# Eight raw weight buffers instead of six, from mixer tiles that share buffers, and the root of the first norm per token in columns of two

## The chip, the cores and the metric

The kernel runs on one core of a Trainium2 chip. Its time is the device time of one execution in microseconds (us); the time that counts is the median of several executions. A core has five engines with a queue of instructions each, which they run in order: PE (matmuls, with its weight loads shown as PEld), DVE and ACT (elementwise work), POOL and SP. Here SP's queue does nothing but issue DMAs, and POOL has almost no work.

## What is computed

One layer of a decoder trunk on 256 tokens of width 2048, all in f32: a SwiGLU feed-forward network (FFN) of inner width 5632, a mixer with two branches, a second FFN, and a final norm. Every sublayer starts with an RMS norm whose gain and shift come from a vector c.

```python
mods = (c_act @ ada_w[l] + ada_b[l]).reshape(b, N_MOD, d)
h = _modulate(x, ffn1_norm[l], mods[:, 0], mods[:, 1])
x = x + 0.5 * mods[:, 2][:, None, :] * _swiglu(h, ffn1_w_gate[l], ffn1_w_up[l], ffn1_w_down[l])
h = _modulate(x, mix_norm[l], mods[:, 3], mods[:, 4])
y = _hybrid_mixer(h, cos, sin, w_in[l], gdn_conv_w[l], gdn_a_log[l], gdn_dt_bias[l], gdn_norm_w[l],
...
x = x + mods[:, 5][:, None, :] * y
h = _modulate(x, ffn2_norm[l], mods[:, 6], mods[:, 7])
x = x + 0.5 * mods[:, 8][:, None, :] * _swiglu(h, ffn2_w_gate[l], ffn2_w_up[l], ffn2_w_down[l])
return _rms_norm(x, final_norm)
```

where `_hybrid_mixer` is a gated delta rule in 8 heads and a sparse attention in 8 heads, merged by gates and projected by w_out, and `_rms_norm` multiplies by rsqrt(mean(x*x) + 1e-6) over the 2048 channels of a token.

## The kernel before

**Layout.** Activations lie transposed: 16 tiles (KT = 16) of 128 channels by 256 tokens, in `xT`. Weights stream from HBM once, nearly 570 MB in all.

**The weight path.** A load puts 512 KB (128 partitions by 1024 f32) into a buffer with the tag `raw`; there are RB = 6 of them, used in turn. Every f32 product is made of three products at the PE's faster f32r type: ACT copies the load to `whi` (L186, L357), DVE subtracts that from the load to give `wlo` (L187, L358), and PE multiplies `whi` with both halves of the activations and `wlo` with the first half (L196, L198; L363 in the blocked form). `whi` and `wlo` have WB = 3 buffers each. The subtraction is the last reader of a raw buffer, so DVE's progress frees it, and the next load into it, which stands in SP's queue, waits for that. The same six buffers serve the gain and shift matrices `ada_w`: two loads of 512 KB for each tile of 128 of their 18432 columns (L241), each read by one DVE multiply-and-sum (L248) that gives a column of `modc`. These are spread between the weights of the first FFN, the mixer and the start of the second FFN by counters (`pace`, `paces`).

**Order.** The code is written for one stream, and a planner of the framework orders each engine's instructions from its own estimate of when operands and buffers are ready. Pools of tiles with a tag and a count of buffers add waits: a tile takes the place of the one that had its tag `bufs` tiles earlier, once that one has been read for the last time.

**The start** (`start`, L426). ACT squares the 16 tiles of x, PE sums them over the channels by a product with ones, 128x256 wide, so each of the 128 partitions holds all 256 tokens' sums. DVE makes the root by an integer guess and three Newton steps (`rsqrt`, L273) on 128x256, while the first 16 `ada_w` loads go through it. Then each tile is modulated (`modulated`, L318) to an `hpair`, and the gate and up weights run in four passes over 4 of the 16 channel tiles each, 22 of 44 units (NS = 22); partial sums lie in `sums`. The other units and the down projections follow with all 16 channel tiles at a time. Later norms, in `Entry.run` and at the end, do it otherwise: sums per token by a product with a column of ones (`token_sums`, L296), the root on 128x2, and two products that carry it back to all 256 columns (`inv_rms`, L302).

**The mixer** has its own pool `mp`. Four groups of two heads run the delta net (`gdn_group`), while projections (`win`, by `proj`) of the next group, and the compression of keys and values (`compress`, tile `cat`), go on beside them; `gdn_out` gates a group's result by way of `sg` into `oA`. Attention follows in two groups (`attend`): keys `kk`, values `vt`, rotated queries `qr`, probabilities `pr`, transposed `pT`. Then `merge_gates` makes the 16 tiles of merge gates from 32 projections. They are put into the buffers of tiles no longer used, by the list `mtags`; AHEAD = 10 of them are made before the up-projections `wup`, the others between those. The planner also places the four stores of x to HBM (`xd`, L571) in SP's queue.

Of the kernel before, what the change touches and what calls it, by code (L numbers as in the profile page):

```python
# [18 lines left out]
F32 = mybir.dt.float32  # L19
# [3 lines left out]
AF = mybir.ActivationFunctionType  # L23
OP = mybir.AluOpType
# [3 lines left out]
P = 128  # L28
S = 256
D = 2048  # L30
KT = D // P
# [4 lines left out]
AB = 33  # L36
H = 8
WB = 3
RB = 6
TB = 6  # L40
MM = 3
NS = 22
# [10 lines left out]
EPS = 1e-6  # L53
# [51 lines left out]
def trunk(tc, a, out, stage=99, dbg=None):  # L105
    nc = tc.nc
    ctx = ExitStack()
    with ctx:
# [5 lines left out]
        def ptile(shape=(P, 512), dt=F32, tag="c", bufs=7 - MM):  # L114
            return psum.tile(list(shape), dt, tag=tag, name=tag, bufs=bufs)
# [14 lines left out]
        ones = cf[:, C_ONE:C_ONE + P]  # L130
# [11 lines left out]
        for hf in range(2):  # L142
            row = wp.tile([1, HC], F32, tag="raw", name="crow", bufs=RB)
            nc.scalar.dma_start(row, a["c"][:, hf * HC:(hf + 1) * HC])
            for q in range(0, HC, 512):
                pt = ptile()
# [126 lines left out]
        def rsqrt(pool, v, tag):  # L273
            sh = list(v.shape)
            y = pool.tile(sh, F32, tag=tag + "y", name=tag + "y", bufs=2)
            t = pool.tile(sh, F32, tag=tag + "t", name=tag + "t", bufs=2)
            nc.vector.tensor_scalar(y.bitcast(I32), v.bitcast(I32), -0.5, float(0x5F3759DF),
                                    op0=OP.mult, op1=OP.add)
            for it in range(3):
                nc.vector.tensor_mul(t, y, y)  # L280
                nc.vector.scalar_tensor_tensor(t, t, 0.25 ** it, v, op0=OP.mult, op1=OP.mult)
                nc.vector.scalar_tensor_tensor(y, t, -3.0, y, op0=OP.add, op1=OP.mult)
            return y


        nrm = ctx.enter_context(tc.tile_pool(name="nrm", bufs=1))
# [15 lines left out]
        def inv_rms(pt):  # L302

            v = nrm.tile([P, 2], F32, tag="v", name="v", bufs=2)
            nc.vector.tensor_scalar(v, pt[:, 0:2], 1.0 / D, EPS, op0=OP.mult, op1=OP.add)
            r = rsqrt(nrm, v, "nr")
            pb = ptile()
            for j in range(2):
                nc.tensor.matmul(pb[:, j * P:(j + 1) * P], r[:, j:j + 1].to_broadcast([P, P]), ident,
                                 start=True, stop=True)  # L310
            return pb[:, :S]
# [113 lines left out]

        def start(fp, n, sizes, wgu, gain):  # L426
            A = nrm.tile([P, KT], F32, tag="A", name="A", bufs=2)
            pt = ptile((P, S))
            for d in range(KT):
                sq = tmp()  # L430
                nc.scalar.activation(sq, xT[:, d], AF.Square)
                nc.tensor.matmul(pt, ones, sq, start=(d == 0), stop=(d == KT - 1))
            hT = []
            sums = [fp.tile([P, 2, S], F32, tag="a", name="gu", bufs=AB) for _ in range(n - RES)]
            pairs = []
            with tc.tile_pool(name="sp", bufs=1) as sp:
                def mods(k0, kb):
                    for m in (1, 0):
                        for d in range(k0, k0 + kb):
                            for _ in ada_cols(m, d, k0 == 0):  # L440
                                yield
                    yield
                    gains(A, gain, 1, slice(k0, k0 + kb))
                    for d in range(k0, k0 + kb):
                        hT.append(modulated(d, rb, A, 0))
                    yield

                def unit(f, subs):
                    if f in kept:
                        ps = kept[f]  # L450
                    elif f >= n - RES:
                        ps = kept[f] = ptile((P, 2, S))
                    else:
                        ps = ptile((P, 2, S), tag="mm", bufs=MM)
                    here = f in kept
                    last = subs[-1][0] + subs[-1][1] == KT
                    for k0, kb in subs:
                        block_rows(ps, (wgu[f],), hT, k0, kb, k0 == (0 if here else subs[0][0]),
                                   k0 + kb == (KT if here else subs[-1][0] + subs[-1][1]))
                    if not here:  # L460
                        if subs[0][0] == 0:
                            nc.scalar.activation(sums[f], ps, AF.Copy)
                        else:
                            nc.vector.tensor_add(sums[f], sums[f], ps)  # L464
                    if last:
                        gu = ps if here else sums[f]
                        s = tmp()
                        nc.scalar.activation(s, gu[:, 0], AF.Silu)
                        nc.vector.tensor_mul(s, gu[:, 1], s)
                        pair = fp.tile([P, 2, S], F32R, tag="a", name="apair", bufs=AB)  # L470
                        split(pair, s)
                        pairs.append(pair)

                kept = {}
                extra = pace(LT, n - 1)
                offs = [[(sum(sum(z) for z in sizes[:b]) + sum(z[:i]), z[i]) for i in range(len(z))]
                        for b, z in enumerate(sizes)]
                for kt, _ in enumerate(mods(*offs[0][0])):
                    if kt == KT - 5:
                        v = nrm.tile([P, S], F32, tag="ssq", name="vb", bufs=1)  # L480
                        nc.vector.tensor_scalar(v, pt, 1.0 / D, EPS, op0=OP.mult, op1=OP.add)
                        rb = rsqrt(sp, v, "rb")
                for b in range(len(sizes)):
                    todo = offs[b + 1] if b + 1 < len(sizes) else []
                    gen = (None for sub in todo for _ in mods(*sub))
                    step = pace(sum(4 * kb + 2 for _, kb in todo), n - LAG)
                    for f in range(n):
                        unit(f, offs[b])
                        for _ in range(step()):
                            next(gen, None)  # L490
                        if b + 1 == len(sizes):
                            ada(extra())
                            if f == n // 2:
                                late_consts()
            return hT, pairs, ()
# [90 lines left out]
        with ExitStack() as mx:  # L586
            mp = mx.enter_context(tc.tile_pool(name="mp", bufs=1))
# [13 lines left out]
            def one(tag="q", bufs=12):  # L601
                return mp.tile([P, S], F32, tag=tag, name=tag, bufs=bufs)
# [12 lines left out]
            nc.vector.tensor_scalar(gnw, V["gnw"], 0.5, None, op0=OP.mult)  # L615


            sm = mp.tile([P, S], F32, name="sm")
            both(win(0), sm)
            tok = mp.tile([P, 2, P], F32, name="tok")  # L620
            ge = mp.tile([P, 2, 2, 8], F32, name="ge")
# [82 lines left out]
            def gdn_group(h0, q, k, v):  # L704
# [14 lines left out]
                def squares(src, acc):  # L719
                    for j in range(4):  # L720
# [3 lines left out]
                pt = flip(k)  # L724
                squares(pt, ss[:, 0])
                kd = big("kd", 2, (P, 2, P))
                nc.vector.tensor_mul(kd, pt[:, 0:2], per(ekd, 0, h0))
                kE = big("kE", 1, (P, 2, P))
                nc.vector.tensor_mul(kE, pt[:, 2:4], per(egc, 1, h0))
                pt = flip(q)  # L730
# [13 lines left out]
                                 skip_group_check=True)  # L744
# [3 lines left out]
                Dt = bt("Dt")  # L748
# [5 lines left out]
                N = bt("N")  # L754
                for j in range(4):
                    nc.vector.scalar_tensor_tensor(N[:, j], pk[:, j], nC[:, j:j + 1], Dt[:, j],
                                                   op0=OP.mult, op1=OP.mult)
# [20 lines left out]
                for lv in range(1, 6):  # L778
# [26 lines left out]
                    if lv == 1:  # L805
                        pt = flip(v)
# [10 lines left out]
                pt = ptile((64, 4, 64))  # L817
                for j in range(4):
                    nc.tensor.transpose(pt[:, j], z[lo, j, lo], ident[lo, lo])
                zq = mp.tile([P, 4, 64], F32, tag="zq", name="zq", bufs=1)  # L820
                nc.scalar.activation(zq[lo], pt, AF.Copy)
                pp = ptile((P, 4, 64))
                for j in range(4):
# [12 lines left out]
                vn = bt("vn")  # L836
                pv = [ptile((P, 2, P)) for _ in range(2)]
                for p in range(2):
                    for i in range(2):
                        nc.tensor.matmul(pv[p][:, i], z[:, 2 * p + i], Vt[:, 2 * p + i], start=(i == 0),  # L840
                                         stop=(p == 0), skip_group_check=True)
# [44 lines left out]
            def gdn_out(h0, oT):  # L886
                for i in range(2):
                    h = h0 + i
                    zg = both(win(W_GZ + h))
                    th = tmp()  # L890
                    nc.scalar.activation(th, zg, AF.Tanh, scale=0.5)
                    sg = mp.tile([P, S], F32, tag="sg", name="sg", bufs=1)
                    nc.vector.scalar_tensor_tensor(sg, th, 1.0, zg, op0=OP.add, op1=OP.mult)
                    sv = sg.rearrange("p (a b) -> p a b", a=2)
                    nc.vector.tensor_mul(sv, sv, v4(oT)[:, :, i])
                    oA[h] = big("oA", 8, (P, 2, S), F32R)
                    split(oA[h], sg)
# [5 lines left out]

            def compress():
                for b in range(2):
                    cat = mp.tile([P, 2, S], F32, tag="cat", name="cat", bufs=2)
                    for g in range(2):
                        both(win(W_KV + 2 * b + g, False), cat[:, g])
                        yield
# [172 lines left out]

            op_ = oA + oB
            yf = []
            mtags = ["kE", "Dt", "N", "o", "vn", "oT", "kd", "kd", "cat", "cat"] + ["pr", "pr", "kk", "kk", "vt", "vt"]
            sgs = []

            def merge_gates(d):
# [3 lines left out]
                nc.scalar.activation(sg, sg, AF.Tanh, scale=0.5)  # L1092
                sgs.append(sg)

            AHEAD = 10
            for d in range(AHEAD):
                merge_gates(d)
            for d in range(KT):
# [124 lines left out]
```

## Time and profile before

| | |
|---|---|
| median of 3 runs | 2404.76 us (2402.72 to 2405.74) |
| profiled execution | 2399.2 us, of it the span from first to last instruction 2397.4 us |
| PE busy | 2301.0 us, 96% of the span |
| DVE busy | 1781.4 us, 74% |
| ACT busy | 1133.5 us, 47% |
| moved by DMA | 571.00 MB, mean 238 GB/s |

In time the kernel is: the start and the blocked passes of the first FFN to about 300 us, the rest of the first FFN to about 800, the delta net to about 1170, attention to about 1295, merge gates, up-projections and w_out to about 1640, the second FFN, and the final norm from about 2370 us.

How to read the rows below. In a row of instructions stand the start in us, the duration in us, engine, line, operation, out<-in, shape and count, and in brackets how long the engine was idle before it and what ended that. SPq and ACTq are the sequencers of those engines, which issue DMAs. A row of waits reads: who waited, for whom, us in total, times, the longest. A busy PE is no PE at its peak, since matmuls overlap in a pipeline; the count of matmuls in a window tells its pace better.

### The profile page before, as it was taken

How to read it: one execution, taken by the hardware profiler on the slowest of the kernel's cores; microseconds unless marked ns; L12 is line 12 of the kernel's file. 1: busy time of each engine (PE TensorE's matmuls, PEld its weight loads, DVE VectorE, ACT ScalarE, POOL GpSimd, SP SyncE). 2: the span in 40 equal slices, each digit the busy share in tenths (PEclk: the TensorE clock that was granted, in tenths of full speed). 3: DMA queues.
4: the chain of work that ended last, by engine and by line, in shares of the span. 5: the costliest groups of instructions: out<-in, count | busy, mean ns of one | idle time of the engine just before them, and what ended most of it. 6: DMA issues, size and time to landing. Idle time of an engine off the chain costs nothing.

```text
span 2397.4 us, 38975 instructions
## 1 busy us (share of the span) xinstructions
PE 2301.0 (96%) x15094; PEld 2029.9 (85%) x15094; DVE 1781.4 (74%) x2896; ACT 1133.5 (47%) x1787; POOL 1.4 (0%) x8
## 2 busy tenths in 40 slices
PE   6999999999999999999999999999999999999997
PEld 4999987887778888887778888889888888888886
DVE  6888877777777797778887778879666666555555
ACT  3433544433444474554545444556544444344453
POOL 0000000000000000000000000000000000000000
PEclk8999999999999999999999999999999999999999
DMA  9988678888888745547676888666777777665663
GB/s 320 319 299 301 199 260 286 285 289 286 273 291 268 245 158 188 170 151 249 226 252 214 284 290 283 214 218 216 232 242 243 241 243 219 192 195 189 184 191 123
DMA packets 174493, 571.00 MB, mean 238 GB/s; under 512 B 17890, under 2 KB 18146, under 8 KB 174308
## 3 DMA queue, kind: packets, MB, share of 16 engines
q1 hardware_dynamic: 173584, 566.09, 72.0%
q8 instruction: 118, 1.93, 0.3%
q10 hardware_dynamic: 724, 2.43, 0.3%
q14 instruction: 67, 0.55, 0.1%
HBM read 564.25 MB, written 4.19 MB: 237 GB/s over the span
## 4 chain that ended last, share of the span: by engine, by line
PE 62%; DMA 17%; DVE 12%; ACT 5%; issue 4%; ACTq 0%; DVEq 0%; SPq 0%
PE mm L196 34%; PE mm L198 18%; DMA raw<-in_w1gu_dram 9%; PE mm L363 5%; DVE wlo L187 4%; DMA raw<-in_win_dram 4%; ACT whi L186 3%; DMA raw<-in_w1d_dram 2%; DVE adaraw L248 2%; PE c L363 2%; DVE wlo L358 1%; ACT whi L357 1%; DMA raw<-in_wup_dram 0%; DVE gu L464 0%; PE c L799 0%
## 5 line engine op out<-in xcount | busy, mean ns | idle before, releaser
L196 PE MATMUL mm<-hpair,whi 128*128 128x512 f32 x3536 | 1249.9, 394 | 17.2 <-ACT whi L186 8.9
L187 DVE TENSOR_TENSOR wlo<-raw,whi 128x1024 fp32r<-128x1024 f32 (+1 forms) x666 | 796.5, 1197 | 485.1 <-ACT whi L186 477.0
L186 ACT ACTIVATE whi<-raw 128x1024 fp32r<-128x1024 f32 (+1 forms) x666 | 690.6, 1038 | 800.3 <-PE mm L196 268.3
L198 PE MATMUL mm<-hpair,wlo 128*128 128x256 f32 x3536 | 1009.4, 286 | 20.7 <-DVE wlo L187 20.2
L196 PEld LDWEIGHTS mm<-hpair,whi 128*128 128x128 f32 x3536 | 667.5, 189 | 161.3 <-ACT whi L186 13.3
L198 PEld LDWEIGHTS mm<-hpair,wlo 128*128 128x128 f32 x3536 | 671.7, 190 | 37.4 <-DVE wlo L187 34.8
L196 PE MATMUL mm<-apair,whi 128*128 128x512 f32 x1408 | 490.2, 391 | 0.8 <-ACT whi L186 0.8
L198 PE MATMUL mm<-apair,wlo 128*128 128x256 f32 x1408 | 398.3, 283 | 2.0 <-DVE wlo L187 1.9
L196 PEld LDWEIGHTS mm<-apair,whi 128*128 128x128 f32 x1408 | 265.1, 188 | 56.5 <-ACT whi L186 1.1
L363 PE MATMUL mm<-hpair,whi 128*128 128x256 f32 x1472 | 262.0, 281 | 17.7 <-ACT hpair L323 16.9
L198 PEld LDWEIGHTS mm<-apair,wlo 128*128 128x128 f32 x1408 | 266.8, 190 | 3.7 <-DVE wlo L187 3.6
L363 PEld LDWEIGHTS mm<-hpair,whi 128*128 128x128 f32 x1472 | 226.1, 189 | 18.8 <-ACT hpair L323 17.3
L363 PE MATMUL mm<-hpair,wlo 128*128 128x256 f32 x736 | 208.4, 283 | 6.9 <-DVE wlo L358 6.7
L248 DVE CUSTOM_DVE_ANT_0 adaraw<-adaraw,cact,vec 128x1024 f32<-128x1024 f32 x144 | 184.0, 1278 | 14.0 <-DMA adaraw<-in_ada_w_dram 14.0
L357 ACT ACTIVATE whi<-raw 128x1024 fp32r<-128x1024 f32 x112 | 118.7, 1060 | 155.9 <-DMA raw<-in_w1gu_dram 87.0
L248 DVE CUSTOM_DVE_ANT_0 adaraw<-adaraw,cact,part 128x1024 f32<-128x1024 f32 x144 | 183.9, 1278 | 0.1
L358 DVE TENSOR_TENSOR wlo<-raw,whi 128x1024 fp32r<-128x1024 f32 x112 | 136.3, 1222 | 43.9 <-ACT whi L357 43.5
L363 PEld LDWEIGHTS mm<-hpair,wlo 128*128 128x128 f32 x736 | 138.9, 189 | 10.8 <-DVE wlo L358 10.3
L222 ACT ACTIVATE t<-mm 128x256 f32<-128x256 f32 x237 | 86.7, 367 | 15.5 <-PE mm L198 15.4
L225 DVE TENSOR_TENSOR t<-mm,t 128x256 f32<-128x256 f32 x193 | 80.7, 418 | 4.8 <-ACT t L222 4.7
L529 DVE SCALAR_TENSOR_TENSOR xT<-mm,g,xT 128x256 f32<-128x256 f32 x128 | 61.5, 481 | 7.1 <-PE mm L198 5.4
L514 ACT ACTIVATE t<-t 128x256 f32<-128x256 f32 x63 | 26.0, 413 | 58.2 <-DVE t L225 58.2
(363 smaller groups left out, 1495.4 us busy)
## 6 DMA issues: line engine op xcount, KB each, us to landing
adaraw<-in_ada_w_dram SPq DMA_DIRECT2D x288, 512.0 KB, 5.6
raw<-in_w2gu_dram SPq DMA_DIRECT2D x180, 512.0 KB, 4.7
raw<-in_w1gu_dram SPq DMA_DIRECT2D x176, 512.0 KB, 5.8
raw<-in_win_dram SPq DMA_DIRECT2D x158, 512.0 KB, 4.8
raw<-in_w1d_dram SPq DMA_DIRECT2D x64, 512.0 KB, 5.2
raw<-in_w2d_dram SPq DMA_DIRECT2D x64, 512.0 KB, 3.5
raw<-in_wup_dram SPq DMA_DIRECT2D x32, 512.0 KB, 4.7
raw<-in_wout_dram SPq DMA_DIRECT2D x32, 512.0 KB, 4.6
```

Of the source, the lines that this page charges most:

```text
L186: nc.scalar.activation(hi[:, :n], raw[:, :n], AF.Copy)
L187: behind(nc.vector.tensor_sub(lo[:, :n], raw[:, :n], hi[:, :n]))
L196: nc.tensor.matmul(ps[:, :], hi, pairs[k][:, :, :].rearrange("p a b -> p (a b)"), start=(k == 0), stop=False, skip_group_check=True)
L198: nc.tensor.matmul(ps[:, S:2 * S], lo, pairs[k][:, 0, :], start=False, stop=(k == n - 1), skip_group_check=True)
L222: nc.scalar.activation(t, ps[:, S:2 * S], AF.Copy)
L225: nc.vector.tensor_add(o, ps[:, :S], t)
L248: nc.vector.tensor_tensor_reduce(out=raw, in0=raw, in1=cact[:, hf * HC:(hf + 1) * HC], scale=1.0, scalar=part[0], op0=OP.mult, op1=OP.add, ...
L357: nc.scalar.activation(hi, raw, AF.Copy)
L358: behind(nc.vector.tensor_sub(lo, raw, hi))
L363: nc.tensor.matmul(ps[:, w], l[:, w, k], h[:, r], start=(first and w == k == x == 0), stop=(last and k == kb - 1 and x == 2), skip_group_c ...
L514: nc.scalar.activation(s, g, AF.Silu, bias=bg)
L529: nc.vector.scalar_tensor_tensor(xT[:, d], pd[:, j * S:(j + 1) * S], g05[:, d:d + 1], xT[:, d], op0=OP.mult, op1=OP.add)
```

## The change

The ring of raw buffers gets eight places instead of six. The space for them comes from the mixer's pool: `sm` becomes one of the twelve `q` tiles, `zq` shares the one buffer of `S`, `sg` the two of `qr` (it had one of its own), and `cat` the two of `kk`. With `cat` gone as a place for merge gates, `pT` takes its part, and only 8 gates instead of 10 go ahead of the up-projections, since `pT` is free only after the attention. In the start, the sums of squares are made per token in two columns (the squares are now the stationary operand, the column of ones moves), and the root goes through `inv_rms` like that of the later norms.

```diff
-RB = 6
+RB = 8
...
-            pt = ptile((P, S))
+            pt = ptile()
             for d in range(KT):
                 sq = tmp()
                 nc.scalar.activation(sq, xT[:, d], AF.Square)
-                nc.tensor.matmul(pt, ones, sq, start=(d == 0), stop=(d == KT - 1))
+                for j in range(2):
+                    nc.tensor.matmul(pt[:, j:j + 1], sq[:, j * P:(j + 1) * P], ones[:, 0:1], start=(d == j == 0),
+                                     stop=(d == KT - 1), skip_group_check=True)
...
-                    if kt == KT - 5:
-                        v = nrm.tile([P, S], F32, tag="ssq", name="vb", bufs=1)
-                        nc.vector.tensor_scalar(v, pt, 1.0 / D, EPS, op0=OP.mult, op1=OP.add)
-                        rb = rsqrt(sp, v, "rb")
+                    if kt == KT // 2:
+                        rb = nrm.tile([P, S], F32, tag="ssq", name="rb", bufs=1)
+                        nc.scalar.activation(rb, inv_rms(pt), AF.Copy)
...
-            sm = mp.tile([P, S], F32, name="sm")
+            sm = one()
...
-                zq = mp.tile([P, 4, 64], F32, tag="zq", name="zq", bufs=1)
+                zq = mp.tile([P, 4, 64], F32, tag="S", name="zq", bufs=1)
...
-                    sg = mp.tile([P, S], F32, tag="sg", name="sg", bufs=1)
+                    sg = mp.tile([P, S], F32, tag="qr", name="sg", bufs=2)
...
-                    cat = mp.tile([P, 2, S], F32, tag="cat", name="cat", bufs=2)
+                    cat = mp.tile([P, 2, S], F32, tag="kk", name="cat", bufs=2)
...
-            mtags = ["kE", "Dt", "N", "o", "vn", "oT", "kd", "kd", "cat", "cat"] + ["pr", "pr", "kk", "kk", "vt", "vt"]
+            mtags = ["kE", "Dt", "N", "o", "vn", "oT", "kd", "kd", "pr", "pr", "kk", "kk", "vt", "vt", "pT", "pT"]
...
-            AHEAD = 10
+            AHEAD = 8
```

Behind the start one line is added, so a line of before has a number smaller by one or two than the same line now.

SP's queue near the end of the first FFN, of before; w1d are weights of the down projection, and xd is the store of four finished tiles of x, which waits for DVE to have made them:

```order
L177 DMA raw<-in_w1d_dram 128x768
L177 DMA raw<-in_w1d_dram 128x1024 x2
L571 DMA xd<-xT 128x1024
L177 DMA raw<-in_w1d_dram 128x768
L177 DMA raw<-in_w1d_dram 128x1024 x2
```

and the same place of the changed kernel:

```order
L177 DMA raw<-in_w1d_dram 128x768
L177 DMA raw<-in_w1d_dram 128x1024 x2
L177 DMA raw<-in_w1d_dram 128x768
L177 DMA raw<-in_w1d_dram 128x1024
L572 DMA xd<-xT 128x1024
L177 DMA raw<-in_w1d_dram 128x1024
```

The store stands two weight loads later in the queue: the loads run two further ahead of the work that they are for.

DVE's queue at the start, of before, from the sum over the second row of `ada_w` loads on (L248 writes part or modc, the root of the norm is vb, rby and rbt):

```order
L248 ISA part 128x1
L481 TENSOR_SCALAR vb<-c 128x256
L248 ISA adaraw,modc<-adaraw,cact,part 128x1024
L248 ISA modc 128x1
L248 ISA adaraw,part<-adaraw,cact,vec 128x1024
L248 ISA part 128x1
L277 TENSOR_SCALAR rby<-vb 128x256
...
L282 SCALAR_TENSOR_TENSOR rby<-rbt,rby 128x256
L320 SCALAR_TENSOR_TENSOR t<-rby,A,xT 128x256 x3
```

and of the changed kernel, where the root is v, nry and nrt and comes to DVE's modulation as rb by way of PE and ACT:

```order
L248 ISA part 128x1
L305 TENSOR_SCALAR v<-c 128x2
L248 ISA adaraw,modc<-adaraw,cact,part 128x1024
L248 ISA modc 128x1
L248 ISA adaraw,part<-adaraw,cact,vec 128x1024
L248 ISA part 128x1
L277 TENSOR_SCALAR nry<-v 128x2
...
L282 SCALAR_TENSOR_TENSOR nry<-nrt,nry 128x2
L248 ISA adaraw,modc<-adaraw,cact,part 128x1024
L248 ISA modc 128x1
L320 SCALAR_TENSOR_TENSOR t<-rb,A,xT 128x256
```

The root starts after five sums instead of seven, works on two columns, and two of the four modulated tiles now come between the last sums instead of behind them.

ACT's queue where the delta net ends and attention begins, of before (qr is the copy for a rotated query, oA the split of a gated head, whose source is sg):

```order
L222 ACTIVATE t<-mm 128x256
L962 ACTIVATE qr<-q 128x256
L186 ACTIVATE whi<-raw 128x1024
L222 ACTIVATE t<-mm 128x256
L186 ACTIVATE whi<-raw 128x1024
L962 ACTIVATE qr<-q 128x256
L186 ACTIVATE whi<-raw 128x1024
L222 ACTIVATE t<-mm 128x256
L883 ACTIVATE oT<-c,gnw 128x512
L186 ACTIVATE whi<-raw 128x1024
L229 ACTIVATE oA<-sg 128x256
```

and of the changed kernel:

```order
L884 ACTIVATE oT<-c,gnw 128x512
L186 ACTIVATE whi<-raw 128x1024
L229 ACTIVATE oA<-sg 128x256 x2
L963 ACTIVATE qr<-q 128x256 x2
L186 ACTIVATE whi<-raw 128x1024
L222 ACTIVATE t<-mm 128x256
```

Two copies of qr that stood ahead of the last group's two splits now stand behind both.

## The prediction

> **What bounds the kernel now.** I read the chain of work that ended last first, because it tells whose lateness sets the end, and after it the busy times of the stages, because the shares of the whole span mix stages with different limits.
>
> ```profile
> PE 62%; DMA 17%; DVE 12%; ACT 5%; issue 4%; ACTq 0%; DVEq 0%; SPq 0%
> PE mm L196 34%; PE mm L198 18%; DMA raw<-in_w1gu_dram 9%; PE mm L363 5%; DVE wlo L187 4%; DMA raw<-in_win_dram 4%; ACT whi L186 3%; DMA raw<-in_w1d_dram 2%; DVE adaraw L248 2%; PE c L363 2%; DVE wlo L358 1%; ACT whi L357 1%; DMA raw<-in_wup_dram 0%; DVE gu L464 0%; PE c L799 0%
> ```
>
> PE leads, but 17% of the chain is a weight load in flight that somebody waits for. The loads named are of the first FFN (w1gu, w1d) and of the mixer (win); those of the second FFN are missing. The stages say the same. Columns are the length, then busy time and count for PE, PEld, DVE, ACT and POOL, the granted clock, the DMA share and GB/s.
>
> ```profile
> 40.00:234.00 194.00, 185.43 (x1516) 180.53 (x1516) 166.27 (x228) 83.73 (x98) 0.00 (x0) 0.99 0.90 304
> 234.00:300.00 66.00, 65.92 (x565) 65.85 (x565) 53.53 (x81) 36.70 (x63) 0.00 (x0) 1.00 0.62 201
> 300.00:800.00 500.00, 475.86 (x2656) 410.11 (x2656) 378.73 (x547) 212.78 (x287) 0.00 (x0) 0.99 0.83 277
> 1090.00:1300.00 210.00, 195.79 (x1396) 165.08 (x1395) 179.62 (x433) 103.43 (x236) 0.00 (x0) 0.98 0.70 234
> 1300.00:1500.00 200.00, 191.53 (x1072) 165.62 (x1072) 151.52 (x215) 89.28 (x126) 0.00 (x0) 0.99 0.84 283
> 1700.00:1800.00 100.00, 100.00 (x579) 88.63 (x578) 68.22 (x92) 49.08 (x73) 0.00 (x0) 1.00 0.75 242
> ```
>
> From 1700 to 1800 us PE never stops and does 579 of the large matmuls in 100 us. At that pace the 2656 of 300 to 800 us need 458.7 us: 41 us are lost there. The 1072 of 1300 to 1500 us need 185.1, so 15 are lost. From 40 to 234 us the matmuls are narrower; 565 in 66 us is their full pace, the 1516 need 177.1, and 17 are lost. From 1090 to 1300 us, where kinds are mixed, PE is idle for 14 us. Busy time alone hides half of this: 475.86 of 500 looks like a loss of 24.
>
> Why PE loses time from 300 to 800 us is in the waits of that stretch; the first four rows are engines, the last the DMA queue of SP (us in total, times, longest).
>
> ```profile
> ACT whi L186 <- DMA raw<-in_w1gu_dram: 122.4, 55, 5.6
> DVE wlo L187 <- ACT whi L186: 118.2, 80, 3.7
> PEld mm L198 <- DVE wlo L187: 25.7, 34, 1.1
> ...
> PEld mm L196 <- ACT whi L186: 12.7, 13, 2.3
> ...
> SPq L177 <- DVE wlo L187: 97.0, 70, 3.0
> ```
>
> PE waits for wlo, DVE for whi, ACT for the load, and SP cannot issue the load before DVE is done with the buffer that it goes into. The circle can be watched once:
>
> ```profile
> 628.06 1.53 SPq L177 DMA_DIRECT2D raw<-in_w1gu_dram  x2
> 630.77 1.43 SPq L241 DMA_DIRECT2D adaraw<-in_ada_w_dram  x2
> 637.51 1.87 SPq L177 DMA_DIRECT2D raw<-in_w1gu_dram  x2
> ...
> 635.17 1.06 ACT L186 ACTIVATE whi<-raw 128x1024 fp32r<-128x1024 f32 x1 [3.72 <-DMA raw<-in_w1gu_dram]
> ...
> 636.26 1.23 DVE L187 TENSOR_TENSOR wlo<-raw,whi 128x1024 fp32r<-128x1024 f32 x1 [3.62 <-ACT whi L186]
> ```
>
> The load issued at 628.06 us is waited for until 635.17; DVE stands still for 3.62 us, frees nothing, and SP issues nothing between about 632 and 637.5 us. It is a loop of six buffers that runs at its own latency, while the DMA engines are 83% busy.
>
> **The ring: six slots to eight.** The page's row of these loads (size, median from issue to landing):
>
> ```profile
> raw<-in_w1gu_dram SPq DMA_DIRECT2D x176, 512.0 KB, 5.8
> ```
>
> 277 GB/s over 500 us are 138.5 MB, 264 loads of 512 KB, one per 1.89 us. Six slots times 1.89 are 11.4 us, the life of a slot from one issue to the next, of which the load is in flight for 5.8. At PE's full pace a load is due every 458.7/264 = 1.74 us, and eight slots then allow a life of 13.9 us: 2.5 us more than now. Said from the other side, each load is issued two loads earlier, 3.8 us, and that is about the longest wait in the example (3.72). SP's rows of the change show that its order does run two loads further ahead (the xd store). So most of the 41 us should go. Not all: where DVE and DMA are most loaded (below) something is late next. I take three quarters, **31 us**; the bounds are 0, if loads land no earlier, and 41.
>
> From 40 to 234 us DMA is at a share of 0.90 already. Its 59 MB at a share of 1 and the same efficiency (304/0.90 = 338 GB/s) take 174.5 us, just under PE's 177.1, so both would bind at once; of 17 I take **8 us**, bounds 0 and 17.
>
> The mixer's two stretches:
>
> ```profile
> ACT whi L186 <- DMA raw<-in_win_dram: 40.6, 24, 5.3
> ...
> ACT whi L186 <- DMA raw<-in_win_dram: 53.7, 18, 5.2
> ```
>
> The first row is of 1090 to 1300 us, the second of 1300 to 1500. The cause is the same, mixed with others (evictions stand behind a wlo in DVE's queue, small matmuls are slow to issue). I take half of the 15 us, **7 us**, bounds 0 and 15, and **5 us** of the 14, bounds 0 and 10. From 234 to 300, 800 to 1090 and after 1500 us nothing waits for loads, and I take nothing.
>
> **The first norm.** Until 38.44 us PE waits for the first modulated tile.
>
> ```profile
> 11.51 9.98 PE L432 MATMUL c<-t,cf 128*128 128x256 f32 x32
> ...
> 25.09 0.29 DVE L277 TENSOR_SCALAR rby<-vb 128x256 int32<-128x256 int32 x1
> ...
> 28.29 2.08 SPq L347 DMA_DIRECT2D raw<-in_w1gu_dram  x2
> ...
> 36.81 0.42 DVE L282 SCALAR_TENSOR_TENSOR rby<-rbt,rby 128x256 f32<-128x256 f32 x1
> 37.36 1.27 DVE L320 SCALAR_TENSOR_TENSOR t<-rby,A,xT 128x256 f32<-128x256 f32 x3
> ...
> 38.44 1.23 PE L363 MATMUL mm<-hpair,whi 128*128 128x256 f32 x2 [16.95 <-ACT hpair L323]
> ...
> 20.00:40.00 20.00, 2.65 (x9) 1.53 (x8) 19.81 (x42) 3.18 (x5) 0.00 (x0) 0.60 0.98 358
> ...
> L280 DVE TENSOR_TENSOR nrt<-nry x9: 160/161/163, 837.5 to 2386.5; 128x2 f32<-128x2 f32 x9
> ...
> 1650.93 0.53 PEld L299 LDWEIGHTS c<-cf,ssq 128*128 128x128 f32 x4
> ```
>
> DVE is busy for 19.81 of 20 us, so its work counts. Eleven wide operations go, ten at about 0.42 and one at 0.29, 4.5 us; eleven on two columns come, at 0.16 each (the root of the later norms, row L280), 1.8 us: 2.7 us less. Two more matmuls and one ACT copy carry the root back to all columns, beside DVE's sums. The squares' sums become 64 recorded passes, at 4 in 0.53 us about 8.5 us against 9.98, so the root is not late, though DVE now asks for it two sums earlier. Half of the modulated tiles also come before the last sums. The first load, now held back by a slot until 28.3 us, may land up to 2.7 us sooner. I take **3 us**, bounds 0 and 5.
>
> **Shared tiles and order in the mixer.** Two rows bound most of these (line, count, min/median/max ns, first and last start).
>
> ```profile
> L852 DVE COPY S<-c x4: 417/418/424, 925.7 to 1154.2; 128x256 f32<-128x256 f32 x4
> ...
> L915 DVE TENSOR_TENSOR G<-cat,vec x4: 948/976/994, 905.8 to 981.1; 128x480 f32<-128x480 f32 x4
> ```
>
> The four S tiles come some 76 us apart, so zq of one group finds S of the group before long read. cat is read for the last time by 982 us, and kk, which takes its place, is of the attention. sm gives its place among twelve q tiles back before the first q tiles do. I cost these at nothing; the group's 76 us of other work are their cover, and without it each of the four groups would wait once, under 0.5 us (the copy). One sharing does bind: sg and qr.
>
> ```profile
> 1166.92 0.42 ACT L962 ACTIVATE qr<-q 128x256 f32<-128x256 f32 x1 [1.43 <-DVE q L225]
> ...
> 1183.26 0.41 DVE L230 TENSOR_TENSOR oA<-sg,oA 128x256 fp32r<-128x256 f32 x1
> ```
>
> Before, the first qr is made at 1166.92 us, while the last sg is read until 1183.67. Now two copies of qr stand behind the two oA splits in ACT's queue, so the first scores come some 2 to 4 us later; behind them wait the softmax's exponentials, and PE has projections to do meanwhile. Its price is between 0 and 17 us; I take 2, near the lower end, because projections follow in PE's order. Eight gates ahead instead of ten only trades places with up-projections: the same loads and matmuls, cost 0, at most 3 us if DVE is late. That leaves 5 - 2 = **3 us** in that stretch.
>
> **Sum**: 31 + 8 + 7 + 3 + 3 = 52 us. The profiled execution took 2399.2 us (span 2397.4), which gives 2347. The median of the runs shown is 5.6 us above it, so I predict 2353 us, 2.2% less.
>
> **A rule weighed.** PE's clock drops now and then:
>
> ```profile
> 360.00:380.00 20.00, 17.07 (x85) 13.96 (x85) 14.61 (x21) 7.93 (x11) 0.00 (x0) 0.91 0.83 275
> ```
>
> This is a window that lost many matmuls (85 instead of 116), and the clock never drops between 1700 and 1800 us, where PE never waits; the mean of 0.99 from 300 to 800 us leaves about 10 us at half pace, three such drops. I count them as part of the 41 us. The Trainium skill, in "TensorE: Matmul & The Clock Gate", Part 1, lets the clock fall after an idle window of about 3.4 us. No single wait for whi or wlo in that stretch is that long (PEld's longest above are 2.3 and 1.1 us); by the page, drops would then have another cause and stay. An estimate by it: three drops of 1.7 us kept, a gain of 47 instead of 52 us. The trace sides with the drops going.
>
> **The rivals.** (1) DVE binds next.
>
> ```profile
> 640.00:660.00 20.00, 17.75 (x98) 14.60 (x97) 15.80 (x24) 8.25 (x12) 0.00 (x0) 1.00 0.82 276
> ```
>
> At 116 matmuls instead of 98, DVE's 15.80 us become 18.7 of 20. It did 19.81 of 20 in the head, but there nothing stood in its queue that had to wait. If it does bind, half of the 46 us from the ring stays lost: gain 29, 2376 us. (2) The DMA engines are full already, and eight loads only queue longer.
>
> ```profile
> 8.00:16.00 8.00, 8.00 (x15) 4.26 (x14) 2.41 (x3) 5.17 (x13) 0.00 (x0) 1.00 1.03 418
> 621.00:624.00 3.00, 1.84 (x11) 1.37 (x10) 0.88 (x4) 0.96 (x1) 0.00 (x0) 1.00 0.95 261
> 633.00:636.00 3.00, 3.00 (x19) 2.65 (x19) 0.00 (x0) 0.83 (x1) 0.00 (x0) 1.00 1.00 392
> ```
>
> Against it: 418 and 392 GB/s when loads queue up, where the stage moves 277. For it: 0.90 in the first stage, 261 at 621 us. Then only the head and some 5 us remain, 2397 us. The Trainium skill, in "DMA: Bandwidth & Descriptors", Specifications, gives about 358 GB/s from HBM for a core; the 418 of the trace is above that, so the measurement decides, and even 358 would carry 138.5 MB in 387 us. (3) Slower: loads in flight get in each other's way, and the engines stay at the 261 GB/s of 621 us however many are queued. From 300 to 800 us, 138.5 MB take 531 us, 31 more; with the head, 2433 us. It decides as soon as full queues yield less than today's 277. (4) The change doesn't do what it says, because the life of a slot grows with their number (buffers freed in the order of DVE's queue): 2402 us, the head alone.
>
> **How the numbers follow.** Forecast 0.60, its own range 2335 to 2372; (1) 0.20; (2) 0.08; (3) 0.08; (4) 0.04. The range reaches from 2328 (nearly all upper bounds, 77 us) to 2390, past (1), and leaves out (2) to (4), 2 in 10. 0.2%, 4.8 us, is about what a measurement of this kernel can tell from no change. Faster by more: the forecast, (1) and (2), 0.88; within it, (4), 0.04; slower 0.08.
>
> **What would show it.** Right: between the same stages ACT's waits for w1gu and win fall to less than a third, the matmul count per 100 us rises towards 579, GB/s in the first FFN rises to about 300, and the first L363 starts near 35 us. Wrong: waits of PE for wlo stay while ACT no longer waits for loads (1); landing takes 3 us longer than the 5.8 of now and the waits stay (2); GB/s falls at a share near 1 (3). A stretch of idle PE near 1185 us would be sg and qr.

## The result and the profile after

| | before | after |
|---|---|---|
| median | 2405.03 us (2402.72 to 2405.74, 4 executions) | 2323.55 us (2323.47 to 2326.03, 4 executions) |
| ratio | | 0.9665, 95% interval 0.9649 to 0.9682 |
| profiled execution, and its span | 2399.2 us, 2397.4 us | 2323.5 us, 2321.6 us |

The change takes off 81 us, 3.4%. The forecast had 52, and its range ended at 2328 us: the direction was right, the size was not. The same shares of the chain that ended last as before, now of the changed kernel:

```profile
PE 90%; DVE 6%; ACT 2%; DMA 1%; issue 1%; DVEq 0%; SPq 0%; ACTq 0%
PE mm L196 48%; PE mm L198 26%; PE mm L363 9%; PE c L363 2%; DVE adaraw L248 1%; DVE wlo L187 1%; DVE wlo L358 1%; DMA raw<-in_win_dram 1%; PE c L433 1%; DMA cf<-in_consts_dram 0%; PE c L1023 0%; ACT whi L186 0%; ACT junk L723 0%; PE c L800 0%; DMA raw<-in_w1gu_dram 0%
```

Loads in flight were 17% of the chain and are 1%; `w1gu` went from 9% to 0%. The stages by the clock of the span, and one window of 20 us in the first FFN (length, then busy time and count for PE, PEld, DVE, ACT and POOL, granted clock, DMA share, GB/s):

```profile
40.00:234.00 194.00, 188.91 (x1583) 187.54 (x1584) 173.32 (x239) 87.19 (x103) 0.00 (x0) 1.00 0.93 323
300.00:800.00 500.00, 499.84 (x2928) 444.72 (x2928) 411.51 (x609) 235.74 (x319) 0.00 (x0) 1.00 0.86 298
640.00:660.00 20.00, 20.00 (x117) 17.74 (x116) 18.24 (x28) 10.24 (x15) 0.00 (x0) 1.00 0.92 324
1090.00:1300.00 210.00, 207.71 (x1254) 179.37 (x1253) 181.98 (x397) 108.54 (x223) 0.00 (x0) 1.00 0.75 258
1300.00:1500.00 200.00, 199.98 (x1149) 176.23 (x1148) 162.49 (x249) 100.39 (x151) 0.00 (x0) 1.00 0.80 277
```

From 300 to 800 us PE now stops for 0.16 us in all, and the loads move at 298 GB/s, one per 1.76 us: PE's own pace, no longer the ring's. The last two rows hold other work than before, since everything there starts 50 to 75 us sooner; they show that PE hardly stops there either. The waits of 300 to 800 us, and in the last row those of 1040 to 1240, the stretch of the mixer that stood at 1090 to 1300 before (us, times, longest):

```profile
ACT whi L186 <- PE mm L196: 126.7, 97, 1.9
DVE wlo L187 <- ACT whi L186: 81.0, 89, 1.8
...
ACT whi L186 <- DMA raw<-in_w1gu_dram: 14.9, 8, 2.4
...
ACT whi L186 <- DMA raw<-in_win_dram: 12.1, 8, 2.5
```

The circle has turned round. ACT's waits for `w1gu` fell from 122.4 us to 14.9, and what ACT waits for most is PE, which has yet to give a `whi` buffer back: the producers now stand behind PE, where that costs nothing. PE's waits for `whi` and `wlo`, 38.4 us in the two rows shown of before, are no longer among the rows. Loads land as they did (median from issue to landing, 5.8 us before):

```profile
raw<-in_w1gu_dram SPq DMA_DIRECT2D x176, 512.0 KB, 5.9
```

One stretch went the other way, the head:

```profile
11.54 14.02 PE L433 MATMUL c<-cf,t 128*128 128x1 f32 x64
...
25.59 0.16 DVE L305 TENSOR_SCALAR v<-c 128x2 f32<-128x2 f32 x1 [6.20 <-PE c L433]
...
34.48 1.22 PE L309 MATMUL c<-cf,nry 128*128 128x128 f32 x4 [8.92 <-DVE nry L282]
...
41.38 0.80 PE L363 MATMUL mm<-hpair,whi 128*128 128x256 f32 x2 [5.68 <-ACT whi L357]
```

The 64 passes over the squares take 14.02 us where the 32 wide ones took 9.98; DVE, which comes to the root early, stands for 6.20 us in front of it, with sums of `ada_w` loads queued behind it. The first matmul of the FFN starts at 41.38 us instead of 38.44.

Where the time went can be read off the starts of the same instructions in both traces. The first column is the start in the profiled execution before, the others are how much earlier the kernel of that column gets there (negative: later). All kernels of the experiments below stand beside the changed one.

```
                       before   after   six   norm   ring  seven   late   wide    DVE
                                       slots  only   only  slots   root   sums   plus
first L363 matmul       38.4    -2.9   -3.1   -3.3    0.7   -2.8    2.4    4.3   -3.0
first L196 matmul      303.6     7.8   -9.7   -8.4   13.0    5.4   11.9   14.5    7.5
last down matmul       833.3    49.5   -7.4  -10.4   54.7   42.3   53.6   56.2   32.2
first attention score 1183.3    54.6  -10.3   -9.9   55.5   34.8   57.9   60.9   29.6
last p*v product      1300.4    62.0   -8.3   -9.8   62.6   41.4   65.3   68.3   28.4
last up-projection    1558.7    75.6  -14.3  -15.8   76.3   55.1   78.9   81.9   37.4
last instruction      2393.4    75.8  -14.8  -15.8   76.3   54.9   79.2   81.9   36.7
```

In the column of after: the head loses 3 us, the four passes gain 10.7, the first FFN from there to its last down product 41.7, the mixer 26.1, and the second FFN nothing. Each column is one execution, and that of before is 5.8 us faster than the median of its kernel; with six slots single stretches also move by some us without another order. In norm only, PE, DVE, ACT and SP run their instructions in the order of before from 300 us on, and yet 6.0 us are lost between the last p*v product and the last up-projection.

### The profile page after: what moved, and what is told of

It reads as the page before. It is cut to its first block, busy times and chain, and to the rows that moved or that the text cites. A ratio compares the mean times of both kernels' runs of the same rounds, so it can differ in the third digit from the quotient of the medians.

```text
span 2321.6 us, 39012 instructions
## 1 busy us (share of the span) xinstructions
PE 2272.6 (98%) x15130; PEld 2028.3 (87%) x15130; DVE 1776.4 (77%) x2896; ACT 1133.3 (49%) x1788; POOL 1.5 (0%) x8
## 4 chain that ended last, share of the span: by engine, by line
PE 90%; DVE 6%; ACT 2%; DMA 1%; issue 1%; DVEq 0%; SPq 0%; ACTq 0%
PE mm L196 48%; PE mm L198 26%; PE mm L363 9%; PE c L363 2%; DVE adaraw L248 1%; DVE wlo L187 1%; DVE wlo L358 1%; DMA raw<-in_win_dram 1%; PE c L433 1%; DMA cf<-in_consts_dram 0%; PE c L1023 0%; ACT whi L186 0%; ACT junk L723 0%; PE c L800 0%; DMA raw<-in_w1gu_dram 0%
## 5 line engine op out<-in xcount | busy, mean ns | idle before, releaser
L196 PE MATMUL mm<-hpair,whi 128*128 128x512 f32 x3536 | 1237.7, 392 | 2.0 <-ACT t L218 2.0
L187 DVE TENSOR_TENSOR wlo<-raw,whi 128x1024 fp32r<-128x1024 f32 (+1 forms) x666 | 796.8, 1196 | 419.3 <-ACT whi L186 417.2
L196 PEld LDWEIGHTS mm<-hpair,whi 128*128 128x128 f32 x3536 | 664.4, 188 | 140.6 <-ACT t L218 2.5
L196 PE MATMUL mm<-apair,whi 128*128 128x512 f32 x1408 | 488.3, 390 | 0.0
L196 PEld LDWEIGHTS mm<-apair,whi 128*128 128x128 f32 x1408 | 264.4, 188 | 55.4
L363 PE MATMUL mm<-hpair,whi 128*128 128x256 f32 x1472 | 260.7, 280 | 5.7 <-ACT whi L357 5.7
L363 PEld LDWEIGHTS mm<-hpair,whi 128*128 128x128 f32 x1472 | 225.9, 189 | 6.0 <-ACT whi L357 6.0
L363 PE MATMUL mm<-hpair,wlo 128*128 128x256 f32 x736 | 207.2, 282 | 3.1 <-DVE wlo L358 3.0
L248 DVE CUSTOM_DVE_ANT_0 adaraw<-adaraw,cact,vec 128x1024 f32<-128x1024 f32 x144 | 183.6, 1275 | 13.2 <-DMA adaraw<-in_ada_w_dram 13.2
L248 DVE CUSTOM_DVE_ANT_0 adaraw<-adaraw,cact,part 128x1024 f32<-128x1024 f32 x144 | 183.8, 1277 | 0.0
L363 PEld LDWEIGHTS mm<-hpair,wlo 128*128 128x128 f32 x736 | 139.2, 189 | 4.2 <-DVE wlo L358 3.8
```

The lines of the kernel that those rows point to most:

```text
L187: behind(nc.vector.tensor_sub(lo[:, :n], raw[:, :n], hi[:, :n]))
L196: nc.tensor.matmul(ps[:, :], hi, pairs[k][:, :, :].rearrange("p a b -> p (a b)"), start=(k == 0), stop=False, skip_group_check=True)
L248: nc.vector.tensor_tensor_reduce(out=raw, in0=raw, in1=cact[:, hf * HC:(hf + 1) * HC], scale=1.0, scalar=part[0], op0=OP.mult, op1=OP.add, ...
L363: nc.tensor.matmul(ps[:, w], l[:, w, k], h[:, r], start=(first and w == k == x == 0), stop=(last and k == kb - 1 and x == 2), skip_group_c ...
```

## The experiments

Two questions: whether the ring alone makes the gain, or the shared tiles and the order of the gates take part; and what the new norm does, which is mixed into every stage after it. Each run has the kernel before timed beside it on the same chip. The first four ran together (before: 2406.43 us, 2396.76 to 2414.72).

**Everything but the ring.** The changed kernel with six slots: the shared tiles, 8 gates and the new norm stay.

```
-RB = 8
+RB = 6
```

> The changed kernel with six raw buffers again; shared tiles, 8 gates ahead and the new root stay. Theory A (the ring alone gives the gain): first matmul of the first FFN near 41 us as in the changed kernel, then 41 us lost between 300 and 800 us and 15 in the merge stretch come back; 2402 to 2412 us. Rival B (part of the mixer's gain, 16 us more than was forecast, comes from the moved order and the 8 gates): 2385 to 2395 us, with the first FFN as slow as before and the mixer faster.

Measured: 2414.96 us, ratio 1.0037 (1.0023 to 1.0051).

```profile
300.00:800.00 500.00, 477.94 (x2696) 413.10 (x2695) 378.86 (x545) 214.35 (x294) 0.00 (x0) 0.99 0.83 277
...
ACT whi L186 <- DMA raw<-in_w1gu_dram: 116.9, 54, 6.1
```

The waits for `w1gu` are back (116.9 us against 122.4 before), and with them PE's stops, the 277 GB/s and a granted clock of 0.99. So the whole gain hangs on the two slots. What is left makes the kernel slightly slower than before, 3 us above the range expected, which the next run places.

**The new norm alone**, in the kernel before (the diff's hunks of the start and nothing else):

```
-            pt = ptile((P, S))
+            pt = ptile()
...
-                nc.tensor.matmul(pt, ones, sq, start=(d == 0), stop=(d == KT - 1))
+                for j in range(2):
+                    nc.tensor.matmul(pt[:, j:j + 1], sq[:, j * P:(j + 1) * P], ones[:, 0:1], start=(d == j == 0),
+                                     stop=(d == KT - 1), skip_group_check=True)
...
-                    if kt == KT - 5:
...
+                    if kt == KT // 2:
+                        rb = nrm.tile([P, S], F32, tag="ssq", name="rb", bufs=1)
+                        nc.scalar.activation(rb, inv_rms(pt), AF.Copy)
```

> The kernel before with only the new root of the first norm. Theory C (the sums in columns leave PE's clock at half, take 14 us and hold DVE up): the first L363 at 41 us or later instead of 38.4, DVE idle about 6 us before v; 2406 to 2411 us. Rival (the forecast's step: less DVE work, sums in 8.5 us): first L363 at 35 to 36 us, 2400 to 2403 us.

Measured: 2414.90 us, ratio 1.0030 (1.0015 to 1.0046), 4 us above the range of the theory and far from the rival's. The norm by itself makes the kernel before about 0.3% slower: the first matmul starts at 41.8 us, 3.3 us late, and the end of the passes is 8.4 us late. Six slots with everything else lie at the same time, 2414.96, so the shared tiles and the 8 gates together cost nothing that these runs show.

**The ring without the norm**: the changed kernel with the old root, the reverse of that diff.

```
-                    if kt == KT // 2:
-                        rb = nrm.tile([P, S], F32, tag="ssq", name="rb", bufs=1)
-                        nc.scalar.activation(rb, inv_rms(pt), AF.Copy)
+                    if kt == KT - 5:
+                        v = nrm.tile([P, S], F32, tag="ssq", name="vb", bufs=1)
+                        nc.vector.tensor_scalar(v, pt, 1.0 / D, EPS, op0=OP.mult, op1=OP.add)
+                        rb = rsqrt(sp, v, "rb")
```

> The changed kernel with the old root of the first norm. Theory C: first L363 at 36 to 38.5 us, the rest as in the changed kernel; 2317 to 2322 us. Rival (the new root helps by 3 us or more): 2326 us or more.

Measured: 2322.52 us, ratio 0.9657 (0.9637 to 0.9677), half a us above the range of the theory. The column "ring only" is 5.2 us ahead of after from the first L196 matmul to the end of the first FFN, as it should be if the norm costs time there; but it loses 4.3 of that between the last down product and the first score. There the granted clock falls once where it doesn't in the changed kernel:

```profile
820.00:840.00 20.00, 17.37 (x98) 15.29 (x99) 16.48 (x37) 13.94 (x38) 0.00 (x0) 0.91 0.35 109
```

That fall isn't the cause: at 860 us of after the lead is 5.6 us, and it is lost from about 930 to 1130 us. Another order isn't either, since PE, DVE, ACT and SP run their instructions in the same order in both kernels from 300 us on. Why the lead is lost stays open. At the end the two differ by no more than the intervals. The norm's cost is seen in its stage, not in the total.

**Seven slots.** Is eight more than needed, and does the gain go with the number of slots?

```
-RB = 8
+RB = 7
```

> The changed kernel with seven raw buffers. Theory A1 (a loop with a fixed life of a slot of 11.4 us: seven slots give a load per 1.63 us, and the full pace needs one per 1.74): nearly all of the gain, 2325 to 2340 us, under 10 us lost from 300 to 800 us. Rival A2 (each slot brings the same): half of it, 2355 to 2370 us.

Measured: 2343.08 us, ratio 0.9737 (0.9717 to 0.9758), a little slower than the first theory's range and far from the second's.

```profile
300.00:800.00 500.00, 496.38 (x2880) 439.55 (x2879) 406.08 (x595) 230.81 (x309) 0.00 (x0) 1.00 0.87 297
...
ACT whi L186 <- DMA raw<-in_w1gu_dram: 50.1, 36, 3.9
...
1080.00:1160.00 80.00, 75.31 (x667) 63.55 (x668) 64.38 (x153) 34.20 (x73) 0.00 (x0) 0.87 0.66 220
```

From the first L196 matmul to the last down product seven slots gain 36.8 us, eight 41.7, six 2.2. That isn't proportional: the seventh slot brings most. In the mixer seven gain 12.6 us where eight gain 26.1. From the first score on the two are nearly alike, 20.3 us against 21.0; the difference lies between the FFN and the first score, where seven lose 7.5 and eight gain 5.1, with the granted clock at 0.87 in the 80 us shown. The two kernels differ in the number of slots and, in that stretch, in the order that the planner makes with it, so which of the two makes this difference can't be told from these runs.

The other four ran together (before: 2402.32 us, 2399.56 to 2409.23), the first of them the changed kernel as it is.

> The changed kernel once more, as the base of this set: 2321 to 2327 us, first L363 near 41.4 us.

Measured: 2323.81 us, ratio 0.9667 (0.9652 to 0.9681): the result repeats to 0.3 us.

**The root asked for later.** If DVE's 6.20 us in front of the sums are the norm's price, a root that stands behind the eleventh of DVE's sums instead of the fifth should not wait:

```
-                    if kt == KT // 2:
+                    if kt == 10:
...
-                        nc.scalar.activation(rb, inv_rms(pt), AF.Copy)
+                        nc.scalar.activation(rb, inv_rms(pt, last_sum[0]), AF.Copy)
...
+            with (tc.issue_after(behind_ins.ins) if behind_ins is not None else ExitStack()):
+                nc.vector.tensor_scalar(v, pt[:, 0:2], 1.0 / D, EPS, op0=OP.mult, op1=OP.add)
```

> The changed kernel, with the root's first operation (v) tied behind the eleventh sum of an ada_w load in DVE's queue. Theory C (DVE stands 6 us for PE's sums, and everything behind it is late by that): no wait of DVE before v over 1 us, first L363 at 34 to 37 us, 2 to 6 us faster than the changed kernel. Rival (the loads bind the blocked passes anyway): first L363 earlier but within 1.5 us of the changed kernel at the end.

Measured: 2320.69 us, ratio 0.9655 (0.9641 to 0.9669), 3.1 us under the changed kernel beside it: 2320.03 to 2321.45 us in four executions, against 2321.42 to 2325.29, though the intervals of the ratios overlap.

```profile
26.95 0.15 DVE L307 TENSOR_SCALAR v<-c 128x2 f32<-128x2 f32 x1
...
36.07 0.80 PE L365 MATMUL mm<-hpair,whi 128*128 128x256 f32 x2 [2.48 <-ACT whi L359]
```

The row of v has no wait in brackets, and the first matmul comes 5.3 us sooner than in after, 2.4 sooner than before. That is near the 2.7 us that the forecast had put for the saving on DVE, but not a measurement of it alone, since the order of DVE's queue in the head differs too.

**The sums made faster.** The same 64 weight loads, but each product runs against all 128 columns of ones instead of one; the root reads one column of each half.

```
-                    nc.tensor.matmul(pt[:, j:j + 1], sq[:, j * P:(j + 1) * P], ones[:, 0:1], start=(d == j == 0),
+                    nc.tensor.matmul(pt[:, j * P:(j + 1) * P], sq[:, j * P:(j + 1) * P], ones, start=(d == j == 0),
...
-                        nc.scalar.activation(rb, inv_rms(pt), AF.Copy)
+                        nc.scalar.activation(rb, inv_rms(pt[:, :S].rearrange("p (a b) -> p a b", a=2)[:, :, 0]), AF.Copy)
```

> The changed kernel, with the sums of squares made against 128 columns of ones instead of one: the same weight loads, wider moving operand. Theory C1 (products with one moving column do not raise PE's clock): clock up near 17 us as in the kernel before, the passes then at 0.11 to 0.13 us instead of 0.213, sums done by 21 us, first L363 at 36 to 38.5 us. Rival C2 (the 64 weight loads take that long at any clock): sums done at 25 us or later as now, first L363 at 41 us or later.

Measured: 2317.89 us, ratio 0.9647 (0.9633 to 0.9662).

```profile
11.70 10.42 PE L433 MATMUL c<-cf,t 128*128 128x128 f32 x64
...
22.44 0.15 DVE L305 TENSOR_SCALAR v<-c 128x2 f32<-128x2 f32 x1
...
34.18 0.80 PE L363 MATMUL mm<-hpair,whi 128*128 128x256 f32 x2 [3.86 <-ACT whi L357]
```

128 times the columns take 3.6 us less, v waits for nothing, and the first matmul comes 7.2 us sooner than in after, a little more than the 6.20 us of DVE's wait. The sums end at 22.1 us, a little after the 21 expected, and the first matmul starts nearly 2 us before its range. This is the fastest kernel of the study: 2317.23 to 2321.45 us in five executions, against 2321.42 to 2325.29 in four of the changed one. It beats before clearly and the changed kernel by about 6 us, though the ends of the ratios' intervals still overlap.

**More work for DVE.** How near was the rival in which DVE binds? A quarter of each `wlo` of L187, which makes those behind the four passes, is subtracted twice; the output doesn't change.

```
+                nc.vector.tensor_sub(lo[:, 0:2], raw[:, 0:2], hi[:, 0:2])
```

> The changed kernel with 256 of the 1024 columns of each wlo subtracted twice, 0.34 us more of DVE for each of 642 loads, 218 us in all. Theory (DVE had room for this change, but little): time is lost only in the first FFN with ada_w loads and in the merge stretch, where DVE was at 17 to 18.4 of 20 us; 15 to 50 us slower than the changed kernel, none lost after 1700 us. Rival (DVE is far from binding): under 5 us.

Measured: 2358.80 us, ratio 0.9815 (0.9799 to 0.9831), 35 us above the changed kernel.

```profile
L187 DVE TENSOR_TENSOR wlo<-raw,whi x666: 392/422/429, 291.7 to 2338.9; 128x256 fp32r<-128x256 f32 x167
...
300.00:800.00 500.00, 489.66 (x2789) 428.98 (x2787) 459.65 (x753) 224.87 (x301) 0.00 (x0) 1.00 0.87 292
1700.00:1800.00 100.00, 100.00 (x579) 88.63 (x578) 80.56 (x128) 49.45 (x73) 0.00 (x0) 1.00 0.74 242
```

In the first FFN DVE goes from 411.51 to 459.65 us of 500, and PE stops for 10 us in these 500; the table shows 17 us lost up to the last down product and 21 more up to the last up-projection, then hardly any. Of the 21, 16 are lost before the last p*v product, in the delta net and the attention, where the theory expected none. The piece added takes 0.42 us each time instead of 0.34. In the second FFN, where DVE is at 80.56 of 100, the additional work is hidden. So DVE had room for this change and for little beyond: in the first FFN, busy for 82% of the stage, it holds PE up nowhere, and at 92% it does.

Not tried: nine or ten slots, and eight slots with `sg` in a buffer of its own.

## Why the forecast was too small

**The mechanism held.** Loads in flight left the chain, ACT's waits for `w1gu` fell to an eighth (less than a third was the sign named), GB/s rose from 277 to 298, and landing stayed at 5.9 us. No rival came true: DVE does 18.24 of 20 us while PE never stops (near the 18.7 forecast for that case), the loads are carried at 323 GB/s in the passes and 298 after them, and PE's stops go with eight slots and come back with six. The step that failed is the sizing of the terms of the sum: the ring's and the mixer's were discounted too far, and the head's had the wrong sign.

**The ring in the first FFN: 31 forecast, 41.7 measured** (from the first L196 matmul to the last down product; the forecast took 300 to 800 us). The 41 us lost were worked out rightly; the discount was wrong. "I take three quarters" rested on "where DVE and DMA are most loaded (below) something is late next", and the rows below show engines that are loaded, but none that would be late once the loads come sooner. Two short windows of the changed kernel, at the times from which the forecast took its slow and its fast stretch of the DMA engines:

```profile
621.00:624.00 3.00, 3.00 (x20) 2.65 (x19) 3.00 (x6) 1.71 (x3) 0.00 (x0) 1.00 0.85 291
633.00:636.00 3.00, 3.00 (x19) 2.69 (x18) 3.00 (x7) 1.75 (x3) 0.00 (x0) 1.00 1.02 410
```

The changed kernel is further on in its work at these times. DVE is busy for 3.00 of 3.00 us in both, and PE too: with eight slots, a DVE that is full for a few microseconds doesn't stop PE. The forecast's own figures said that the ring meets the pace: a life of 11.4 us for a slot, 13.9 allowed by eight at 1.74 us per load. Seven allow 12.2, also more than 11.4, and the run with seven gained 36.8 of the 41.7. The 4.9 us that seven slots leave, and the eighth takes, may be single loads that come later than the average; no run shows that.

**The mixer: 10 forecast, 26.1 measured.** The forecast took 7 of 15 and 5 of 14 us of lost time, less 2 for sg and qr. Up to the first score 5.1 us were gained, in the attention 7.4, and from there to the last up-projection 13.7, nearly all that the bounds held. The 2 us for sg and qr can't be found: the first copy of qr now waits for an oA split, but for 0.2 us. How much of the 26.1 is the planner's other order stays open. The 13.7 are the same to 0.1 us in every eight-slot kernel but the one with more work for DVE, and with seven slots. The 5.1 are less firm: ring only, with the same order of instructions from 300 us on, gains 0.8 in that stretch.

**The passes: 8 forecast, 10.7 measured**, well inside 0 to 17. In one window of the passes the DMA share reaches 1.01 at 359 GB/s without PE stopping:

```profile
80.00:100.00 20.00, 20.00 (x170) 19.80 (x170) 18.64 (x25) 13.09 (x19) 0.00 (x0) 1.00 1.01 359
```

**The head: +3 forecast, -2.9 measured, outside its bounds of 0 to 5.** The saving on DVE may have been right (2.7; the first matmul is 2.4 us early where the root comes late enough). "4 in 0.53 us about 8.5 us" for the sums was wrong: that row is from 1650 us, behind dense matmuls, and at 11 us a pass takes 0.22 us instead of 0.13. The forecast also saw that DVE asks for the root two sums earlier and wrote that "the root is not late"; with the sums 5.5 us longer than priced, it was, by 6.20 us. 2.7 - 6.2 = -3.5, close to the -2.9 measured. Both cures, a later root and faster sums, turned the sign.

**The sum and the range.** 52 against 75.8: -6 from the head, +3 from the passes, +11 from the FFN, +16 from the mixer. A further 5.6 us came from the last line, where the profiled execution's distance to the median was added: before scatters by that much, while the changed kernel's profiled execution lies at its median. The low end, 2328 us, allowed for 77 us of gain and then added those 5.6; without them it would have been 2322 and held the result. All its upper bounds together were 88 us, and the change took off 81.

**The rule on the clock.** By the rule of the Trainium skill that the forecast weighed ("TensorE: Matmul & The Clock Gate", Part 1: the clock falls after an idle window of about 3.4 us), the drops had another cause than these short waits and would have stayed. They went: the granted clock of 300 to 800 us is 1.00 with seven and eight slots, and 0.99 with six, before as in the changed kernel with its ring undone. The traces' records of the clock have three falls of 3.4 us each in that stretch with six slots (before at 372, 440 and 679 us) and none with seven or eight. In the 7 us ahead of each of the three falls of before, PE was idle two or three times, never for more than 2.03 us at once.

## What to carry to other kernels

When a ring of load buffers bounds a stage, compare the life of a slot with slots times the pace that the consumer needs: if the pace is then met, book the whole loss as the likely gain (eight slots, with 13.9 us against 11.4, took it all; seven, with 12.2, took nine tenths), and discount it only for an engine that a row shows to be late while others wait for it. Take an operation's price from a row with the same kind of work ahead of it, and when an edit lets a consumer ask earlier, check when the thing asked for is ready. A range that must hold a discounted sum has to include the sum without discounts.

## What the runs showed of the hardware

Products with one moving column didn't bring PE up to pace. In slices of 2 us, the sums alone (PE and PEld busy and count, granted clock, DMA share, GB/s), first of wide sums, 128 columns:

```profile
16.00:18.00 2.00, 2.00 (x12) 2.00 (x12) 1.00 1.03 410
18.00:20.00 2.00, 2.00 (x20) 2.00 (x20) 1.00 1.02 408
```

and of the changed kernel, one column:

```profile
16.00:18.00 2.00, 2.00 (x11) 2.00 (x11) 1.00 1.03 412
18.00:20.00 2.00, 2.00 (x11) 2.00 (x11) 1.00 1.02 408
```

With 128 columns the pace nearly doubles after about 6 us of such work; with one it stays for all 14 us. The column of the granted clock reads 1.00 in all four, but the traces' records of the clock begin only with the rise to full: at 17.8 us in wide sums, and at 48.6 us in after, where two products of L363 with `whi` take 0.63 us up to 48.0 and 0.40 from 48.7 on. In all ten traces it goes with the width: the three kernels with sums of 128 or 256 columns have the rise at 16.8 to 17.8 us, during the sums, and the seven with one column at 45.4 to 50.8 us, when the FFN's products have run for some us. The Trainium skill, in "TensorE: Matmul & The Clock Gate", Part 1, has the full clock come after about 3.4 us of sustained matmuls; the one-column products kept PE busy without a gap for four times that and stayed slow, so being busy without a gap wasn't enough here.
